# Triangular masks by position on GpSimd instead of multiplications on VectorE and ScalarE

## The chip, the cores and the metric

The kernel runs on one core of a Trainium2 chip. Time is device time in microseconds (us) from start to end of one execution. Engines are named as in the profile: PE (TensorE matmul), PEld (its weight load), DVE (VectorE), ACT (ScalarE), POOL (GpSimd), SP (SyncE, which issues most DMAs).

## The reference

The reference is a trunk of two layers over a sequence of 512 tokens with 1024 features, in float32. Layer 0 mixes tokens with an RWKV-7 recurrence, layer 1 with a gated block mixer; each is followed by a SwiGLU feed-forward net. The change touches the recurrence alone:

```python
def _rwkv7_scan(r, w, k, v, a, b):
    # S_t = S_{t-1} diag(w_t) + (S_{t-1} a_t) b_t^T + v_t k_t^T ;  y_t = S_t r_t
    def step(S, inp):
        r_t, w_t, k_t, v_t, a_t, b_t = inp
        sa = jnp.einsum('bhij,bhj->bhi', S, a_t)
        S = (S * w_t[:, :, None, :]
             + sa[..., None] * b_t[:, :, None, :]
             + v_t[..., None] * k_t[:, :, None, :])
        y = jnp.einsum('bhij,bhj->bhi', S, r_t)
        return S, y
...
x = x + _rmsnorm(h, norm_gains[i, 1])
```

There are 16 heads of 64 features. The kernel doesn't step through 512 tokens; it cuts them into 8 chunks of 64. Inside a chunk, what token s gives to token t is a product of two 64x64 tiles of which only the part with s before t counts (or s up to t, for the output). These products have to be masked to a triangle, and a unit triangular matrix has to be inverted.

## The kernel before, in words

The trunk runs recurrence, feed-forward, mixer, feed-forward in one program. The recurrence works on four blocks b of four heads. A list of stages at line 33, `PLAN`, sets in which order they are written: projections P, E (decay and scaled keys), then for each block F (front), B (back), S (scan of the state over the chunks) and N (norm, gate). The text order isn't the order of execution: the framework schedules all instructions with a model of their times, engine by engine, so a changed instruction can move others.

**front(b)** (line 677) handles four units, one per half of the chunks and pair of heads, and in each both heads. For a head it makes four products of 128x128 (L708, tile `lm`) into one PSUM bank; there are two such banks in turn, which `bkt` shares. `lm` holds for four chunks the two products, 64 by 2 by 64 values on 64 rows each for "other" (the rows of the other head) and "rows" (its own). From this bank four things are read: L711 multiplies the rows of the other head by the mask `mk2` (0 and 1; strict triangle for the first product, with the diagonal for the second) into the tile `MV` on DVE; L714 copies the upper part of the own rows' first product into `LA` on ACT in two copies of 32 rows, where the rest was zeroed ahead by POOL (L694); L715 copies the second product into `BX`. After both heads L716 multiplies that part of `BX` by the mask with the diagonal, on DVE. Then four transposes into `bkt` (L721) are copied to `BX` by ACT (L725, L726).

**back(b)** (line 729) transposes `LA` in blocks of 32 on DVE into `LX` (L734), and ACT scales a part of `LA` by a column of the mask, 0 or 1 per row (L739), beside POOL's zeroing of another part (L741). DVE then runs an elimination of 15 steps (L747, L749) on `LX` and `Dm` and transposes its result (L752, L753). From there small products on PE (`Qp` L769 first, which reads the changed `LA`, then `Np`, `Tp`, `Q2p`, `T2p`) put the inverse together, `mp` and `gh` apply it to `MV` and `BX` (L810, L817), and DVE adds the results into `MV` (L819, L820).

The mask is built at the start by one memset and four selects on POOL (L404 to L408). A select (`affine_select`) keeps an element where a linear function of its row and of its place in the row passes a comparison, and writes a constant elsewhere.

Of the kernel before, what the change touches and what calls it, by code (L numbers as in the profile page):

```python
# [7 lines left out]
F32 = mybir.dt.float32  # L8
F32R = mybir.dt.float32r
I32 = mybir.dt.int32  # L10
AF = mybir.ActivationFunctionType
ALU = mybir.AluOpType

P = 128
# [5 lines left out]
C = 64  # L20
# [62 lines left out]
class Trunk:  # L83
# [287 lines left out]
    def rwkv(self, x0, nxt):  # L371
        nc, i, tc = self.nc, self.i, self.tc
        v, a, g = nc.vector, nc.scalar, nc.gpsimd
        mm = nc.tensor.matmul
        with ExitStack() as ctx:
            ep = ctx.enter_context
            rp = ep(tc.tile_pool(name="rp", bufs=1))
# [12 lines left out]
            def e2(name, shape=(P, 2, T), dt=F32):  # L390
                return rp.tile(list(shape), dt, name=name, tag="e2", bufs=E2)

            def s4(name, shape, dt=F32):
                return self.slot(shape, dt, name)
# [5 lines left out]
                return self.gp.tile(shape, F32, name=name, tag="gain", bufs=2)  # L400


            mk2 = rp.tile([P, 2, C], F32, name="mk2")
            g.memset(mk2, 1.0)  # L404
            for r in (0, 64):
                for j, op in ((0, ALU.is_gt), (1, ALU.is_ge)):
                    g.affine_select(out=mk2[r:r + 64, j, :], in_=mk2[r:r + 64, j, :], compare_op=op,
                                    fill=0.0, base=0, pattern=[[1, C]], channel_multiplier=-1)  # L408
            rmask = rp.tile([P, NC, C], mybir.dt.bfloat16, name="rmask")
            g.memset(rmask, 1.0)  # L410
            g.memset(rmask[:, :, 0:1], 0.0)
# [85 lines left out]
            for t, m, w in ((w1m[0], omix, v), (w1m[1], self.vec["mix"], g)):  # L497
                mv = m[:, 3 * KT:5 * KT].rearrange("p (j k) -> p k j", j=2).unsqueeze(3)
# [109 lines left out]
            def early(b, k, r):  # L608
# [65 lines left out]
                        nc.sync.dma_start(out=sb[b][head[hd], :, :, n, :].rearrange("p q c t -> p (q c) t"), in_=sv(t)[head[hd]])  # L674
                return dict(pc=pc, BN=BN)

            def front(b, o):

                MV, ST, BX = {}, {}, {}
                for hh in range(2):  # L680
                    st = ST[hh] = e2("ST", (P, 2, 4, 2, C))
                    nc.sync.dma_start(out=st.rearrange("p q c n t -> p q (c n t)"),
                                      in_=sb[b][:, :, 4 * hh:4 * hh + 4].rearrange("p q c n t -> p q (c n t)"))
                    for q in q2:
                        mv = MV[hh, q] = s4("MV", [P, 2, 4, 2, C])
                        for hd in range(2):
                            g.memset(mv[head[1 - hd], :, :, hd], 0.0)
                            for n in range(2):
                                nc.sync.dma_start(out=mv[head[hd], n, :, hd],
                                                  in_=sa[b][n, head[hd], q, 4 * hh * C:4 * hh * C + 4 * C].rearrange("p (c t) -> p c t", t=C))  # L690
                LA = e2("LA", (P, 2, NC, C))
                Dm = self.f0p.tile([P, 2, 528], F32, name="Dm", tag="f0", bufs=2)
                for hd in range(2):
                    g.memset(LA[64 * hd + 32:64 * hd + 64, :, :, 0:32], 0.0)  # L694
                g.memset(full(Dm), 0.0)
                g.memset(Dm.rearrange("p b r -> p (b r)")[:, 0:1024:33], 1.0)
                for hh, q in units:
                    st, mv = ST[hh][:, q], MV[hh, q]

                    bx = BX[hh, q] = s4("BX", [P, 4, 4, C])  # L700
                    for hd in range(2):
                        nc.sync.dma_start(out=bx[head[hd], 2 + hd],
                                          in_=self.ident[head[hd], head[hd]].unsqueeze(1).broadcast_to([64, 4, C]))
                    for hd in range(2):
                        rows, other = head[hd], head[1 - hd]
                        lm = self.bank("pl", "lm")
                        for cc in range(4):
                            mm(lm[:, cc * P:(cc + 1) * P], st[:, cc].rearrange("p n t -> p (n t)"), mv[:, :, cc, hd, :], start=True, stop=True)  # L708
                        lv = lm.rearrange("p (c a t) -> p c a t", c=4, a=2)
                        la = LA[:, q, 4 * hh:4 * hh + 4]  # L710
                        v.tensor_tensor(mv[other, :, :, hd].rearrange("p a c t -> p c a t"), lv[other],  # L711
                                        mk2[other].unsqueeze(1).broadcast_to([64, 4, 2, C]), op=ALU.mult)
                        for z, x in ((64 * hd, 0), (64 * hd + 32, 32)):
                            a.copy(la[z:z + 32, :, x:C], lv[z:z + 32, :, 0, x:C])  # L714
                        a.copy(bx[rows, 1], lv[rows, :, 1, :])  # L715
                    v.tensor_tensor(bx[:, 1], bx[:, 1], mk2[:, 1:2, :].broadcast_to([P, 4, C]), op=ALU.mult)  # L716

                    sf = st.rearrange("p c n t -> p c (n t)")
                    pt = self.bank("pl", "bkt")
                    for cc in range(4):  # L720
                        nc.tensor.transpose(pt[:, cc * P:(cc + 1) * P], sf[:, cc], self.ident)  # L721
                    pv = pt.rearrange("p (c h f) -> p c h f", c=4, h=2)
                    for hd in range(2):
                        rows, other = head[hd], head[1 - hd]
                        a.copy(bx[rows, 0], pv[rows, :, hd])  # L725
                        a.copy(bx[other, 2 + hd], pv[other, :, hd])  # L726
                o.update(MV=MV, BX=BX, LA=LA, Dm=Dm)

            def back(b, o):

                MV, BX, LA, Dm = (o[n] for n in ("MV", "BX", "LA", "Dm"))
# [3 lines left out]
                LAu = LA.rearrange("p q c t -> p (q c) t")  # L735

                for r in (0, 64):
                    for z, x in ((r, 0), (r + 32, 32)):
                        a.activation(LAu[z:z + 32, :, x + 16:x + 32], LAu[z:z + 32, :, x + 16:x + 32], AF.Copy,  # L739
                                     scale=mk2[z:z + 32, 0, x + 16:x + 17])  # L740
                        g.memset(LAu[z:z + 32, :, x:x + 16], 0.0)  # L741
                LXd, Dmd = diag(LX), diag(Dm)
                for j in range(15):
                    n = 15 - j
# [53 lines left out]
                for u in range(16):  # L798
                    for hd in q2:
                        z = 64 * hd  # L800
                        mm(T2p[z:z + 32, u * 32:(u + 1) * 32], Q2[z + 32:z + 64, u, :], bdT[z + 32:z + 64, u, hd, 32:64],
                           start=True, stop=True)
                for hd, cp in ((0, a.copy), (1, v.tensor_copy)):
                    z = 64 * hd
                    cp(bdT[z:z + 32, :, hd, 32:64], T2p[z:z + 32, :].rearrange("p (u t) -> p u t", t=32))

                for hh, q in units:
                    mp, mt, mv, bx = self.bank("mp" if b else "pt", "mp"), MVt[hh, q], MV[hh, q], BX[hh, q]
# [4 lines left out]
                    for hd in range(2):  # L813
                        rows, other = head[hd], head[1 - hd]
# [132 lines left out]
            for n in PLAN:  # L947
                f, b = n[0], int(n[1])
                if f == "P":
                    if xr is None:  # L950
                        xr = mixed_split(0, "ssssssss")
                        xx.clear()
                    kr[b] = kr_proj(b)
                elif f == "E":
                    ops[b] = early(b, *kr[b])
                elif f == "X":
                    xs = mixed_split(2, XV)
                elif f == "V":
                    v_proj(xs, [b])
                elif f == "F":  # L960
                    front(b, ops[b])
                elif f == "B":
                    back(b, ops[b])
                elif f == "S":
                    if b == 3:
                        GW.append(gate_weights(b))
                        OB.extend(bonus(b, ops[b]))
                    Y[b] = scan(b, ops[b], (lambda y: finish_half(b, ops[b], y, (0, 1))) if b == 3 else None)
                elif b == 3:
                    finish_half(b, ops[b], Y[b], (2, 3))  # L970
                else:
                    finish(b, ops[b], Y[b])
# [166 lines left out]
```

## Time and profile before

| what | value |
|---|---|
| time, 3 runs | 1393.85 us (1392.23 to 1398.0) |
| the profiled execution: its time, its span | 1395.72 us, 1394.0 us |
| mean granted TensorE clock | 0.971 |
| PE, PEld, DVE, ACT, POOL busy | 1332.0, 1088.7, 783.9, 579.2, 152.6 us |
| first to last of the edited lines of the fronts and backs | some 187 to 352 us |

A row of a group reads: line, engine, operation, tile written <- tiles read, shapes, count | busy us in all, mean ns of one | idle time of the engine just before them and what ended it. In a timeline the first two numbers are start and length in us. A table by windows has for each stretch its length, then busy us and count for each engine asked for.

### The profile page before, as it was taken

Reading aid. Unit: us, or ns where it says so; the run is one execution under the profiler, and the core shown is the slowest. Engines: PE = TensorE matmul, PEld = TensorE weight load, DVE = VectorE, ACT = ScalarE, POOL = GpSimd, SP = SyncE. Lnnn points to the kernel's source line nnn. Section 1 sums busy time; section 2 is a strip of 40 time slices with the busy share of each in tenths; the row PEclk is TensorE's granted clock in tenths of the full one; section 3 lists DMA queues with packets and bytes.
Section 4 is the critical chain, followed back from the end, with each engine's and each line's share of the span. In section 5 each row is a group of like instructions: output and inputs, shape, how many; then the busy total and the mean of one; then the engine's idle time right before and its main releaser. Section 6 shows DMA issues by size and latency. Waiting matters only on the chain.

```text
span 1394.0 us, 21544 instructions
## 1 busy us (share of the span) xinstructions
PE 1332.0 (96%) x8512; PEld 1088.7 (78%) x8512; DVE 783.9 (56%) x1373; ACT 579.2 (42%) x1076; POOL 152.6 (11%) x190
## 2 busy tenths in 40 slices
PE   5999979989799899999999999999999999999998
PEld 3677768878687688888888887878888888888886
DVE  7975776579847565544553225575574554453223
ACT  5665765566543453222322224543463332232121
POOL 5000200111000021111110002010121111110000
PEclk8999979989799999999999999999999999999999
DMA  5145375432214233333322332342223333332231
GB/s 150 36 140 148 108 208 166 127 77 69 92 49 158 61 101 112 91 95 102 91 91 91 103 109 76 107 138 89 91 77 93 103 91 93 103 92 91 91 105 61
DMA packets 209956, 142.00 MB, mean 102 GB/s; under 512 B 59536, under 2 KB 185024, under 8 KB 209856
## 3 DMA queue, kind: packets, MB, share of 16 engines
q1 hardware_dynamic: 208560, 135.91, 33.0%
q0 software_dynamic: 1296, 4.72, 1.0%
q8 instruction: 67, 1.10, 0.3%
q14 instruction: 33, 0.27, 0.1%
HBM read 124.35 MB, written 14.16 MB: 99 GB/s over the span
## 4 chain that ended last, share of the span: by engine, by line
PE 62%; DVE 2%; ACT 0%; issue 0%; DVEq 0%
PE gu L157 12%; PE gu L158 12%; PE gu L156 11%; PE acc L157 8%; PE acc L158 8%; PE acc L156 8%; PE u L158 1%; PE u L157 1%; PE u L156 1%; DVE x L273 1%; PE s L1065 1%; PE ptr L218 0%; DVE hT L59 0%; DVE rt L208 0%; DVE ry L209 0%; DVE hn L270 0%
## 5 line engine op out<-in xcount | busy, mean ns | idle before, releaser
L131 ACT CAST whi<-wraw 128x1024 fp32r<-128x1024 f32 x177 | 185.7, 1049 | 481.3 <-PE gu L157 250.5
L132 DVE TENSOR_TENSOR wlo<-wraw,whi 128x1024 fp32r<-128x1024 f32 x177 | 263.1, 1487 | 206.3 <-ACT whi L131 202.3
L156 PE MATMUL gu<-hT,whi 128*128 128x512 f32 (+1 forms) x768 | 288.8, 378 | 1.8 <-ACT hT L57 1.7
L157 PE MATMUL gu<-hT,whi 128*128 128x512 f32 (+1 forms) x768 | 288.5, 377 | 1.1 <-DVE hT L59 1.1
L158 PE MATMUL gu<-hT,wlo 128*128 128x512 f32 (+1 forms) x768 | 289.5, 378 | 0.0
L156 PEld LDWEIGHTS gu<-hT,whi 128*128 128x128 f32 x768 | 145.0, 190 | 31.5 <-ACT hT L57 2.3
L157 PEld LDWEIGHTS gu<-hT,whi 128*128 128x128 f32 x768 | 144.9, 189 | 30.5 <-DVE hT L59 1.5
L158 PEld LDWEIGHTS gu<-hT,wlo 128*128 128x128 f32 x768 | 145.1, 189 | 28.5 <-issue 0.2
L157 PE MATMUL acc<-wlo,act 128*128 128x512 f32 x416 | 164.0, 394 | 0.0
L156 PE MATMUL acc<-whi,act 128*128 128x512 f32 x416 | 163.5, 394 | 0.0
L158 PE MATMUL acc<-whi,act 128*128 128x512 f32 x416 | 160.4, 394 | 0.0
L332 DVE TENSOR_TENSOR sg<-sg,gu 128x512 f32<-128x512 f32 x44 | 30.3, 688 | 142.2 <-PE gu L158 139.2
L333 POOL TENSOR_TENSOR sg<-sg,hn 128x512 f32<-128x512 f32 x44 | 57.0, 1295 | 417.3 <-DVE sg L332 417.3
L156 PEld LDWEIGHTS acc<-whi,act 128*128 128x128 f32 x416 | 78.2, 188 | 18.1
L158 PEld LDWEIGHTS acc<-whi,act 128*128 128x128 f32 x416 | 78.2, 188 | 18.0
L157 PEld LDWEIGHTS acc<-wlo,act 128*128 128x128 f32 x416 | 78.1, 188 | 18.0
L330 DVE TENSOR_TENSOR sg<-gu,hn 128x512 f32<-128x512 f32 x44 | 30.4, 691 | 66.5 <-PE gu L158 66.3
L131 ACT CAST act<-sg 128x512 fp32r<-128x512 f32 x52 | 32.3, 621 | 71.7 <-POOL sg L333 57.5
L156 PE MATMUL proj<-xsp,whi 128*128 128x512 f32 x128 | 51.6, 403 | 0.0
L158 PE MATMUL proj<-xsp,wlo 128*128 128x512 f32 x128 | 51.1, 401 | 0.0
L157 PE MATMUL proj<-xsp,whi 128*128 128x512 f32 x128 | 50.3, 396 | 0.2 <-DVE xsp L132 0.2
L708 PE MATMUL lm<-MV,ST 128*128 128x128 f32 x256 | 40.0, 309 | 7.0 <-ACT BX L726 3.0
(303 smaller groups left out, 2124.0 us busy)
## 6 DMA issues: line engine op xcount, KB each, us to landing
wraw<-in_ffn_w_gate_dram SPq DMA_DIRECT2D x44, 512.0 KB
wraw<-in_ffn_w_up_dram SPq DMA_DIRECT2D x44, 512.0 KB, 3.8
wraw<-in_ffn_w_down_dram SPq DMA_DIRECT2D x44, 512.0 KB, 3.7
wraw<-in_rwkv_w_rkv_dram SPq DMA_DIRECT2D x24, 512.0 KB, 3.7
wraw<-in_sgu_w_in_dram SPq DMA_DIRECT2D x16, 512.0 KB, 3.7
x<-in_x_dram SPq DMA_DIRECT2D x8, 512.0 KB, 3.2
MV<-sa SPq DMA_DIRECT2D x64, 64.0 KB, 2.5
ST<-sb SPq DMA_DIRECT2D x8, 512.0 KB
```

The source lines that it names most:

```text
L131: self.nc.scalar.copy(hi, src)
L132: self.nc.vector.tensor_tensor(lo, src, hi.bitcast(F32), op=ALU.subtract)
L156: mm(out, lhs[0], rhs[0], start=start, stop=False)
L157: mm(out, lhs[0], rhs[1], start=False, stop=False)
L158: mm(out, lhs[1], rhs[0], start=False, stop=stop)
L273: v.scalar_tensor_tensor(xts[tt][:, c], f, y[:, 0:1], xts[tt][:, c], op0=ALU.mult, op1=ALU.add)
L330: nc.vector.tensor_tensor(sg, pp[0], yb, op=ALU.mult)
L332: nc.vector.tensor_tensor(sg, sg, pp[1], op=ALU.mult)
L333: nc.gpsimd.tensor_tensor(sg, sg, yb, op=ALU.mult)
L708: mm(lm[:, cc * P:(cc + 1) * P], st[:, cc].rearrange("p n t -> p (n t)"), mv[:, :, cc, hd, :], start=True, stop=True)
L1065: mm(acc[:, tt * P:(tt + 1) * P], vt[tt][:, m * P:(m + 1) * P], wsT[:, m, :], start=True, stop=True)
```

## The change

The tile `mk2` and what built it are gone. A helper, `upper`, selects on POOL by position, in place in SBUF: of 64 rows with four groups of 64 elements it keeps the triangle and writes 0 elsewhere. ACT now copies all of the `lm` bank without mask, 64 rows each: the other head's rows into `MV` (128 values in four chunks), the own rows into `LA` and `BX`. POOL then selects in `MV` twice (each product), in `LA` and in `BX`, once for each head. In the back the scaling by a mask column on ACT is a select on POOL, of 32 rows by 256 elements.

```diff
@@ rwkv
-            mk2 = rp.tile([P, 2, C], F32, name="mk2")
-            g.memset(mk2, 1.0)
-            for r in (0, 64):
-                for j, op in ((0, ALU.is_gt), (1, ALU.is_ge)):
-                    g.affine_select(out=mk2[r:r + 64, j, :], in_=mk2[r:r + 64, j, :], compare_op=op,
-                                    fill=0.0, base=0, pattern=[[1, C]], channel_multiplier=-1)
...
+            def upper(t, base):
+
+                g.affine_select(out=t, in_=t, compare_op=ALU.is_ge, fill=0.0, base=base, pattern=[[0, 4], [1, C]],
+                                channel_multiplier=-1)
+
@@ front
-                for hd in range(2):
-                    g.memset(LA[64 * hd + 32:64 * hd + 64, :, :, 0:32], 0.0)
...
-                        v.tensor_tensor(mv[other, :, :, hd].rearrange("p a c t -> p c a t"), lv[other],
-                                        mk2[other].unsqueeze(1).broadcast_to([64, 4, 2, C]), op=ALU.mult)
-                        for z, x in ((64 * hd, 0), (64 * hd + 32, 32)):
-                            a.copy(la[z:z + 32, :, x:C], lv[z:z + 32, :, 0, x:C])
+                        a.copy(mv[other, :, :, hd].rearrange("p a c t -> p c a t"), lv[other])
+                        for n in range(2):
+                            upper(mv[other, n, :, hd], n - 1)
+                        a.copy(la[rows], lv[rows, :, 0, :])
+                        upper(la[rows], -1)
                         a.copy(bx[rows, 1], lv[rows, :, 1, :])
-                    v.tensor_tensor(bx[:, 1], bx[:, 1], mk2[:, 1:2, :].broadcast_to([P, 4, C]), op=ALU.mult)
+                        upper(bx[rows, 1], 0)
@@ back
-                        a.activation(LAu[z:z + 32, :, x + 16:x + 32], LAu[z:z + 32, :, x + 16:x + 32], AF.Copy,
-                                     scale=mk2[z:z + 32, 0, x + 16:x + 17])
+                        later = LAu[z:z + 32, :, x + 16:x + 32]
+                        g.affine_select(out=later, in_=later, compare_op=ALU.is_ge, fill=0.0, base=15,
+                                        pattern=[[0, 16], [0, 16]], channel_multiplier=-1)
                         g.memset(LAu[z:z + 32, :, x:x + 16], 0.0)
```

The line numbers of the changed kernel are lower by 2 to 6: the copies are L708 (MV), L711 (LA) and L713 (BX), the select is L673, LX is L732, the select of the back L738, the elimination L746 and L748.

The scheduler puts the instructions in another order. On ACT, in the first front, each read of a product waited for DVE before (number of the buffer behind each name; in brackets the semaphores waited for):

```order
L714 COPY LA_1510<-lm_1519 32x256 [waits DMAHW6_49,DVE_49]
L714 COPY LA_1510<-lm_1519 32x4x32
L715 COPY BX_1516<-lm_1519 64x256
L649 ACT_TABLE_LOAD
L649 ACTIVATE tw_1351<-tw_1351 128x1024 [waits Activation_49]
L725 COPY BX_1516<-bkt_1538 64x256 [waits PE_49]
L726 COPY BX_1516<-bkt_1538 64x256
L725 COPY BX_1516<-bkt_1538 64x256
L726 COPY BX_1516<-bkt_1538 64x256
L714 COPY LA_1510<-lm_1528 32x256 [waits DVE_49]
```

Now the first read of a bank waits for PE itself, and for POOL, which zeroed the tile MV:

```order
L708 COPY MV_1474<-lm_1511 64x4x2x64 [waits PE_49,Pool_49]
L711 COPY LA_1504<-lm_1511 64x256 [waits DMAHW6_49]
L713 COPY BX_1508<-lm_1511 64x256
L708 COPY MV_1474<-lm_1523 64x4x2x64 [waits PE_49,Pool_49]
L711 COPY LA_1504<-lm_1523 64x256
L713 COPY BX_1508<-lm_1523 64x256
```

Both heads' products of a unit are read on end, three copies for each; ACT waits for no engine but PE and POOL there.

On POOL the first front had nothing to do but zeroing; the last rows of it and the first of the back stood so:

```order
L694 MEMSET LA_1510 32x16x32 [waits DMAHW6_49,DVE_49,Pool_49]
L694 MEMSET LA_1510 32x16x32
L695 MEMSET Dm_1511 128x1024 [waits DMAHW0_49,DMAHW3_49,DVE_49,DMAHW5_49,Activation_49,Pool_49]
...
L741 MEMSET LA_1510 32x16x16 [waits DVE_49]
L741 MEMSET LA_1510 32x16x16 [waits Activation_49]
```

Now the end of that front and the start of the back read, in POOL's own order:

```order
L673 AFFINE_SELECT BX_1580<-BX_1580 64x256 [waits Activation_49]
L692 MEMSET Dm_2093 128x1024 [waits DVE_49,PE_49,Pool_49]
L693 MEMSET Dm_1505 128x32
L673 AFFINE_SELECT MV_1497<-MV_1497 64x4x64 [waits Activation_49,Pool_49]
L673 AFFINE_SELECT MV_1497<-MV_1497 64x4x64
L673 AFFINE_SELECT LA_1504<-LA_1504 64x256 [waits Activation_49]
L673 AFFINE_SELECT BX_1616<-BX_1616 64x256 [waits Activation_49]
...
L673 AFFINE_SELECT BX_1616<-BX_1616 64x256 [waits Activation_49]
L738 AFFINE_SELECT LA_1504<-LA_1504 32x16x16 [waits DVE_49]
L740 MEMSET LA_1504 32x16x16
```

A memset of the next block's Dm (Dm_2093) stands among the selects of the first block, and the selects of the last head lie ahead of the back's.

On DVE, around the LX of the last block, masks stood on both sides of it:

```order
L752 STREAM_TRANSPOSE hn<-Dm 128x32x32
L753 STREAM_TRANSPOSE Dt<-Dm 128x32x32
L716 TENSOR_TENSOR BX<-BX,mk_128 128x256
L711 TENSOR_TENSOR MV<-lm,mk_128 64x4x2x64
L848 TENSOR_TENSOR su<-us,pc 64x2x64
L132 TENSOR_TENSOR g2l<-g_4780,g2h 128x256
L711 TENSOR_TENSOR MV<-lm,mk_128 64x4x2x64
L772 TENSOR_TENSOR Qs<-Qp,id_147 128x512
L734 STREAM_TRANSPOSE LX<-LA 128x1024
L875 TENSOR_REDUCE mu<-Y 128x16
L716 TENSOR_TENSOR BX<-BX,mk_128 128x256
L132 TENSOR_TENSOR wlo<-wraw,whi 128x1024
```

Now the same place reads:

```order
L751 STREAM_TRANSPOSE hn<-Dm 128x32x32
L752 STREAM_TRANSPOSE Dt<-Dm 128x32x32
L847 TENSOR_TENSOR su<-us,pc 64x2x64 x3
L771 TENSOR_TENSOR Qs<-Qp,id_141 128x512
L132 TENSOR_TENSOR g2l<-g_4846,g2h 128x256
L847 TENSOR_TENSOR su<-us,pc 64x2x64
L732 STREAM_TRANSPOSE LX<-LA 128x1024
L746 TENSOR_TENSOR tm<-LX,Dm 128x2x15
L748 TENSOR_TENSOR Dm<-Dm,tm 128x2x15
L746 TENSOR_TENSOR tm<-LX,Dm 128x2x28
```

No mask is left, and the elimination starts directly behind LX.

## The prediction

> **What bounds the kernel now.** I read the page first, then the chain of waits, then a table by stretches of time.
>
> ```profile
> span 1394.0 us, 21544 instructions
> PE 1332.0 (96%) x8512; PEld 1088.7 (78%) x8512; DVE 783.9 (56%) x1373; ACT 579.2 (42%) x1076; POOL 152.6 (11%) x190
> PE 62%; DVE 2%; ACT 0%; issue 0%; DVEq 0%
> ```
>
> TensorE is busy for 96% of the span, and it alone makes up nearly all that the chain followed back from the end shows. So a mask that another engine does can only be worth the time in which TensorE stands still, or runs at a low granted clock, because of it. The table by stretches says where that is (columns: length, then busy time and instructions of PE, PEld, DVE, ACT and POOL, granted clock, DMA share, GB/s).
>
> ```profile
> 185.00:215.00 30.00, 22.46 (x152) 20.26 (x151) 23.20 (x30) 18.12 (x44) 3.28 (x7) 0.77 0.75 201
> 215.00:262.00 47.00, 43.86 (x744) 42.45 (x744) 25.51 (x55) 23.80 (x52) 2.32 (x6) 0.93 0.39 123
> 262.00:313.00 51.00, 45.28 (x793) 40.28 (x791) 36.86 (x82) 35.10 (x93) 10.02 (x22) 0.90 0.45 116
> 313.00:348.00 35.00, 33.39 (x425) 28.33 (x424) 31.63 (x90) 23.01 (x66) 4.75 (x12) 1.00 0.28 68
> 348.00:380.00 32.00, 24.09 (x412) 19.98 (x411) 28.60 (x67) 17.02 (x31) 1.22 (x4) 0.68 0.31 96
> 505.00:1394.00 889.00, 878.56 (x3978) 717.61 (x3978) 422.50 (x620) 291.08 (x462) 88.46 (x68) 1.00 0.31 95
> ```
>
> From 505 us on TensorE is busy for 878.6 of 889 us at a clock of 1.00, and no edited line runs there: nothing is to be had. The edited work lies in 185 to 380, the fronts and backs of the four blocks. Two places have slack on TensorE. In 185 to 215 (the first front) it is idle for 7.5 of 30 us, at a clock of 0.77. In 313 to 380 (the last front and back) DVE is the fullest engine, 60.2 of 67 us, and TensorE is idle for 1.6 us ahead of 348 and 7.9 us behind it. Between them, 215 to 313, TensorE is busy for 89.1 of 98 us and no other engine is near full.
>
> **The change part by part.** The groups of 185 to 380, by shape, carry the durations (count, then busy us, mean ns, idle before and what ended it):
>
> ```profile
> L711 DVE TENSOR_TENSOR MV<-lm,mk 64x512 f32<-64x512 f32 x32 | 22.0, 687 | 9.0 <-PE lm L708 8.4
> L716 DVE TENSOR_TENSOR BX<-BX,mk 128x256 f32<-128x256 f32 x16 | 6.7, 417 | 4.8 <-ACT BX L715 4.8
> L714 ACT COPY LA<-lm 32x256 f32<-32x256 f32 x32 | 11.6, 361 | 21.7 <-DVE MV L711 21.4
> L714 ACT COPY LA<-lm 32x128 f32<-32x128 f32 x32 | 8.2, 258 | 0.4
> L715 ACT COPY BX<-lm 64x256 f32<-64x256 f32 x32 | 11.8, 367 | 3.0 <-DVE MV L819 2.1 <-PE Yp L859 0.2 <-PE v L158 0.2
> L725 ACT COPY BX<-bkt 64x256 f32<-64x256 f32 x32 | 11.7, 365 | 5.4 <-PE bkt L721 5.4
> L763 ACT COPY MVt<-mvt 128x512 f32<-128x512 f32 x12 | 6.9, 584 | 2.7 <-PE mvt L760 1.6 <-PE gh L817 0.9
> L739 ACT ACTIVATE LA<-LA,mk 32x256 f32<-32x256 f32 x16 | 8.1, 505 | 2.9 <-DVE LX L734 2.7
> L741 POOL MEMSET LA<- 32x256 f32 x16 | 4.9, 305 | 37.7 <-DVE LX L734 37.1
> L687 POOL MEMSET MV<- 64x512 f32 x16 | 8.3, 521 | 44.7 <-DVE MV L819 34.9 <-PE Yp L859 9.2 <-PE v L158 0.2
> ```
>
> DVE loses both masks: 22.0 + 6.7 = 28.7 us. ACT loses L714 (11.6 + 8.2) and L739 (8.1), 27.9 us. It gains 32 copies of 64x256 into LA, at L715's 0.367 us 11.7 us, and 32 copies of 64x512 into MV, which L763's copy of the same length prices at 0.584: 18.7 us. ACT ends 2.5 us heavier, but no longer stands behind DVE's masks for 21.4 us (the L714 row).
>
> GpSimd gets 128 selects of 64x256 and 16 of 32x256, and loses small memsets. The only selects in this trace are at its start:
>
> ```profile
> L407 POOL TENSOR_SCALAR_AFFINE_SELECT mk<-mk 64x64 f32<-64x64 f32 x4 | 0.8, 235 | 0.0
> masks.py:199 POOL TENSOR_SCALAR_AFFINE_SELECT ident<-ident 128x128 f32<-128x128 f32 x1 | 0.3, 285 | 0.1
> L404 POOL MEMSET mk<- 128x128 f32 x1 | 0.2, 202 | 0.0
> ```
>
> From 64 to 128 elements a row a select grows by 50 ns, 0.78 ns an element, so one of 256 takes 285 + 128 x 0.78 = 385 ns; I take 0.39. The lower bound is that of the memset of 256, 0.305 (L741). The upper bound is that each of the four rows of 64 in the new pattern costs a select of its own, 4 x 0.235 = 0.94. 0.39 is what two rows of the same instruction give, so I stay with it: 144 x 0.39 = 56 us of GpSimd, in a stretch of 195 us in which it was busy for 3.28 + 2.32 + 10.02 + 4.75 + 1.22 = 21.6.
>
> **First front, 187.2 to 212.9.** The chain here runs lm product, mask on DVE, three copies on ACT, and back for the next of two banks:
>
> ```profile
> 186.26 1.95 PE L708 MATMUL lm<-MV,ST 128*128 128x128 f32 x16
> 192.91 3.75 PE L708 MATMUL lm<-MV,ST 128*128 128x128 f32 x16 [3.04 <-ACT BX L726]
> 187.19 1.06 ACT L648 ACTIVATE tw<-tw 128x1024 f32<-128x1024 f32 x1 [1.70 <-DVE tw L647]
> 189.18 1.28 ACT L649 ACT_TABLE_LOAD   x1
> 204.61 1.05 ACT L131 CAST whi<-wraw 128x1024 fp32r<-128x1024 f32 x1
> 212.87 2.05 DVE L734 STREAM_TRANSPOSE LX<-LA 128x1024 f32<-128x1024 f32 x1 [0.77 <-ACT LA L714]
> ```
>
> Now ACT alone sets the pace. Per product 0.584 + 0.367 + 0.367 = 1.32 us, eight of them 10.5; 16 copies of bkt at 0.366, 5.9; two activations of 1.06, one table load of 1.28 and two casts of 1.05, 5.5: 21.9 us. Behind the last copy GpSimd has two selects of MV, which run beside ACT's copy of LA, and one of LA: some 0.8 us. So LX starts 22.7 us behind 187.2 instead of 25.7: 3 us gained, within the 7.5 us in which TensorE is idle. The v products that filled the holes of this front come later now, under the elimination on DVE that follows; I count no gain and no loss for them.
>
> **Middle, 215 to 313.** The ACT waits vanish too, but no wait of TensorE hangs on them but once (3.04 us, above). I count nothing; the bound is the 8.9 us in which TensorE is idle.
>
> **Last front and back, 313 to 380.** Asked by line, the two masks are there with
>
> ```profile
> 313.00:380.00 67.00, 6.18 (x9) 0.85 0.29 81
> 313.00:380.00 67.00, 2.08 (x5) 0.85 0.29 81
> 314.57 1.95 DVE L734 STREAM_TRANSPOSE LX<-LA 128x1024 f32<-128x1024 f32 x1
> 348.47 1.96 DVE L734 STREAM_TRANSPOSE LX<-LA 128x1024 f32<-128x1024 f32 x1
> 374.42 2.08 DVE L752 STREAM_TRANSPOSE hn<-Dm 128x1024 f32<-128x1024 f32 x1
> ```
>
> so 8.3 us of the fullest engine go. All but 0.4 us of it lies ahead of the LX at 348.5, and there TensorE is idle for 1.6 us only: LX comes 1.6 us earlier, more only if products move behind it. Behind LX the elimination shares DVE with the norm of the earlier blocks, and some rows of block 2 that stood ahead of LX now follow it; neither shrinks. I take 2 us of the 8.3.
>
> **The rest.** After the LX transpose four selects and four memsets alternate on GpSimd, 4 x (0.39 + 0.305) = 2.8 us, where ACT's four activations took 4 x 0.505 = 2.0 us. The reader is the Qp product behind the elimination, some 30 us later (LX at 348.5, its transposes at 374.4): hidden; without that cover it would be 0.8 us a block. The five instructions that built the mask, 4 x 0.235 + 0.202 = 1.1 us, lie on GpSimd ahead of any product: nothing. What queues behind a waiting select on GpSimd is the next block's memsets of Dm and MV, and LX, the one tight reader, waits behind both.
>
> **Sum.** 3 + 0 + 2 = 5 us off the profiled execution's 1395.72 us (1.7 us of it outside the span of 1394.0). That execution is 1.9 us above the median, 1393.85, so the time is 1393.85 - 5 = **1389 us**.
>
> **Two engines at one memory.** This speaks against the change: other GpSimd instructions that read SBUF held DVE up, or were held up by it. Below them stand DVE's two lines of the elimination in 313 to 380 (L747, then L749).
>
> ```profile
> 525.26 1.92 DVE L132 TENSOR_TENSOR wlo<-wraw,whi 128x1024 fp32r<-128x1024 f32 x1 [0.54 <-ACT whi L131]
> 524.80 1.30 POOL L333 TENSOR_TENSOR sg<-sg,hn 128x512 f32<-128x512 f32 x1 [7.50 <-DVE sg L332]
> L132 DVE TENSOR_TENSOR wlo<-wraw,whi x177: 1201/1226/2377, 18.7 to 1366.1; 128x1024 fp32r<-128x1024 f32 x177
> L77 POOL TENSOR_SCALAR hn<-ident,y x12: 599/610/1540, 499.5 to 1029.8; 128x128 f32<-128x128 f32 x12
> 313.00:380.00 67.00, 7.42 (x30) 0.85 0.29 81
> 313.00:380.00 67.00, 7.48 (x30) 0.85 0.29 81
> ```
>
> The split that takes 1.226 us at the median took 1.92 beside a GpSimd product that ran from 524.80 to 526.10, and a one-input GpSimd instruction of 0.610 reached 1.540 us. No select ran beside DVE in this trace, so its case is unseen. Bounds for 313 to 380: 9 of the 32 masks of L711 stand there, so 9/32 x 128 = 36 selects, and 8 more of two backs, 44 x 0.39 = 17.2 us. At one end nobody waits; at the other DVE waits for all 17.2. About half of the work left to DVE there could be touched at all: the elimination's 14.9 us read two tiles of SBUF (LX or Dm with tm), while the six transposes, some 12 us, read one, and the products with mp, gh and us read a product of TensorE. Part of the waiting would fall on GpSimd instead, as in L77's row. So I take a fourth, 4 us, and it comes out of the 8.3 - 2 = 6.3 us of DVE's relief that I have not counted: it costs nothing. The Trainium skill, page "SBUF — State Buffer", section "Who interferes with whom", states that a DVE instruction with two SBUF inputs and a GpSimd instruction that reads SBUF shut each other out, one blocked until the other is done; the lengthened split agrees, and by that rule the elimination's 60 instructions would be the ones to lengthen.
>
> **The rivals.**
>
> *The full relief comes out.* DVE's 8.3 us all shorten 313 to 380, because products of TensorE move behind LX into the 7.9 us of idling there, and the clock of 0.68 rises with it. With 3 us of the front and a third of the middle's 8.9, 14 us: **1380**. For it: DVE is busy for 31.63 of 35 and 28.60 of 32 us, more than ACT by 8 and 11. Against it: TensorE's 33.39 of the same 35 us.
>
> *Selects hold DVE up.* In 313 to 380 its two-input instructions wait for them: 17.2 - 8.3 = 9 us more where DVE is fullest, and the first front's 3 us go the same way: **1403**. It decides from 8.3 / 0.39 = 21 of the 44 selects, if each holds DVE for its whole length. For it: the rows above. Against it: the half of DVE's work that reads one tile.
>
> *A select costs 0.94 us.* In the first front 32 of them take 30 us, where the front took 25.7: 4 us lost. Between the last two LX, 348.47 - 314.57 = 33.9 us, GpSimd would have 36 x 0.94 + 12 memsets (4 x 0.305 and 8 x 0.521, 5 in all) = 39 us: 5 more lost. With no relief left, 9: **1403**. It decides from (33.9 - 5) / 36 = 0.80 us a select. Against it: two rows with the same instruction.
>
> *Nothing moves.* The front's 3 us is work of TensorE that only shifts, so the total of its products sets the time: **1394**.
>
> **How the numbers follow.** A difference of 0.5%, 7 us, is about what a measurement of this kernel can tell from none: faster means below 1386.9, slower above 1400.8. Chances: forecast 0.37, full relief 0.34, selects that hold DVE up 0.15, costly selects 0.06, nothing moves 0.08. Of the forecast's share 0.05 falls below 1386.9. Faster: 0.34 + 0.05 = 0.39. Same: 0.32 + 0.08 = 0.40. Slower: 0.15 + 0.06 = 0.21. The range goes from 1377, 3 us below the full relief, to 1407, 4 above the two slower cases; I leave 0.1 out on each side, full relief with more of the idle time in it below, and the slower cases together above. The forecast's own range is 1385 to 1394.
>
> **What would show it.** Selects of 64x256 near 0.39 us. No ACT copy waiting for a DVE mask, against 21.4 us. The first block's LX some 23 us behind the activation of tw that stands at 187.19, against 25.7, and TensorE idle for less than 7.5 us in that front. The last block's LX 3 to 5 us earlier in all, and from it to the elimination's end as long as now. L747 and L749 at a mean of 0.25 us as now (7.42 / 30); at 0.35 or more the selects hold DVE up. If the stretch that is now 505 to the end is not 889 us long, something other than these steps is in it. The forecast is wrong if LX waits for GpSimd by more than 2 us in a block, or if the last Qp comes over 8 us earlier.

## The result, and the profile after

The changed kernel is slower: 1409.21 us median of five executions (1403.7 to 1412.82) against 1396.79 for the kernel before (1392.23 to 1398.0), a ratio of 1.0098 with a 95% interval of 1.008 to 1.0116, some 13 us. The profiled execution of it took 1403.7 us, the fastest of its five (granted clock 0.974, the others 0.968 to 0.971), so the traces show 8 us of the difference, not all of it.

First the page of the changed kernel, then its table by stretches (the columns are those of the table in the prediction).

```profile
span 1402.0 us, 21623 instructions
PE 1330.4 (95%) x8512; PEld 1087.2 (78%) x8512; DVE 766.0 (55%) x1325; ACT 579.2 (41%) x1060; POOL 215.5 (15%) x321
```

```profile
0.00:185.00 185.00, 165.19 (x787) 120.07 (x788) 139.39 (x215) 112.45 (x182) 27.51 (x53) 0.99 0.42 117
185.00:215.00 30.00, 21.79 (x158) 18.42 (x157) 16.05 (x17) 23.70 (x50) 22.02 (x36) 0.89 0.79 214
262.00:313.00 51.00, 42.30 (x712) 37.67 (x710) 32.29 (x76) 33.87 (x87) 26.96 (x64) 0.90 0.48 121
313.00:348.00 35.00, 34.21 (x442) 29.89 (x441) 23.52 (x60) 20.18 (x53) 17.39 (x45) 0.90 0.24 60
348.00:380.00 32.00, 23.98 (x453) 20.25 (x453) 24.57 (x63) 18.67 (x38) 8.11 (x19) 0.75 0.27 85
505.00:1402.00 897.00, 885.13 (x4041) 723.61 (x4039) 427.82 (x652) 299.66 (x493) 92.02 (x72) 1.00 0.31 95
```

The relief is there: DVE has 23.52 us of work from 313 to 348 where it had 31.63, and ACT stands behind no DVE mask. GpSimd now works for 22 of 30 us in the first front. But the first row is the one to look at. Ahead of 185 us no mask is applied in either kernel, and yet TensorE was busy there for 165.19 us with 787 products (clock 0.99), in the kernel before for 168.81 with 792 (clock 0.95):

```profile
0.00:185.00 185.00, 168.81 (x792) 123.43 (x793) 138.71 (x215) 114.46 (x184) 28.57 (x60) 0.95 0.44 123
```

When the same step starts in the two profiled executions, by their timelines (us):

| step | before | changed | later by |
|---|---|---|---|
| first v product (the projections are done) | 156.7 | 160.5 | 3.8 |
| first lm product | 186.3 | 188.0 | 1.7 |
| LX of the four blocks | 212.9, 269.8, 314.6, 348.5 | 213.8, 272.3, 316.3, 354.1 | 0.9, 2.5, 1.7, 5.6 |
| Qs of the last block | 393.7 | 397.5 | 3.8 |
| last gh product ends | 426.5 | 434.8 | 8.3 |
| first gu product (the feed-forward net) | 487.7 | 496.0 | 8.3 |

From there to the end of the last product both take the same time, 899.6 and 899.2 us. So the loss lies ahead of 435 us, in several pieces, and some of it where nothing was edited but the order.

The new instructions themselves, in groups and in the waits of 185 to 400:

```profile
L673 POOL TENSOR_SCALAR_AFFINE_SELECT MV<-MV 64x256 f32<-64x256 f32 x64 | 29.9, 489 | 73.4 <-ACT MV L708 73.1
L673 POOL TENSOR_SCALAR_AFFINE_SELECT LA<-LA 64x256 f32<-64x256 f32 x32 | 15.7, 492 | 2.0
L673 POOL TENSOR_SCALAR_AFFINE_SELECT BX<-BX 64x256 f32<-64x256 f32 x32 | 14.7, 459 | 21.2 <-ACT BX L713 20.9
L738 POOL TENSOR_SCALAR_AFFINE_SELECT LA<-LA 32x256 f32<-32x256 f32 x16 | 10.1, 632 | 4.4 <-DVE LX L732 3.5
```

```profile
DVE LX L732 <- POOL LA L673: 6.9, 3, 4.4
```

GpSimd waits for ACT most of the time (73.1 us ahead of the selects of MV). LX waits for a select for 6.9 us in all. That is a wait that was not there before, so selects and order are two suspects.

### The profile page after: what moved, and what is told of

Its sections match the earlier page's. It is cut to its first block, busy times and chain, and to the rows that moved or that the text cites. A ratio compares the mean times of both kernels' runs of the same rounds, so it can differ in the third digit from the quotient of the medians.

```text
span 1402.0 us, 21623 instructions
## 1 busy us (share of the span) xinstructions
PE 1330.4 (95%) x8512; PEld 1087.2 (78%) x8512; DVE 766.0 (55%) x1325; ACT 579.2 (41%) x1060; POOL 215.5 (15%) x321
## 4 chain that ended last, share of the span: by engine, by line
PE 80%; DVE 7%; DMA 5%; ACT 4%; issue 3%; SPq 1%; POOL 0%; DVEq 0%; ACTq 0%; POOLq 0%
PE gu L158 11%; PE gu L156 11%; PE gu L157 11%; PE acc L156 9%; PE acc L157 8%; PE acc L158 8%; PE gh L816 2%; PE proj L156 2%; PE proj L158 2%; PE proj L157 2%; PE mp L809 1%; PE lm L705 1%; PE u L158 1%; PE u L157 1%; PE u L156 1%
## 5 line engine op out<-in xcount | busy, mean ns | idle before, releaser
L156 PE MATMUL proj<-xsp,whi 128*128 128x512 f32 x128 | 52.2, 412 | 0.9 <-ACT r L522 0.9
L148 POOL TENSOR_TENSOR wlo<-wraw,whi 128x1024 fp32r<-128x1024 f32 x12 | 29.0, 2420 | 138.1 <-ACT whi L147 138.1
```

The source lines that it names most:

```text
L148: nc.gpsimd.tensor_tensor(lo, raw, hi.bitcast(F32), op=ALU.subtract)
L156: mm(out, lhs[0], rhs[0], start=start, stop=False)
```

## The experiments

Theory A: the loss comes from the order in which the scheduler put all engines' instructions once a few of them had changed. Theory B: it comes from the selects, by their time on GpSimd, by LX waiting for them, by DVE held up by them.

To tell them apart, an order has to be held while the work changes. A few lines do that: behind the building of the program, each instruction of an engine gets an edge to the one that is to stand ahead of it. The edge sets the order of issue and waits for nothing. The table holds the places of the wanted order. Each run below has a ratio to the kernel before, timed beside it on the same chip; its median moved between 1395.5 and 1397.8 us from chip to chip, so a difference in us between two runs on different chips is good to some 2 us at best.

```diff
+def _pin(nc, tc, table):
+    ...
+    dep = mybir.DependencyInfo(mybir.DependencyClass.NoSync, mybir.DependencyReason.DATA)
+    for engine, steps in order.items():
+        at, last = 0, None
+        for s in steps:
+            at += s
+            i = per[engine][at]
+            if last is not None:
+                tc.add_manual_dep(i, last.name, dep, reason="order")
+            last = i
...
     with tile.TileContext(nc, schedule_with_timeline_sim=True) as tc:
         build(tc, ins, outs[0])
+        _pin(nc, tc, _ORDER)
```

### The work of the one in the order of the other

The changed kernel in the old order (`_ORDER` from the kernel before, for PE, DVE, ACT and SP):

> The changed kernel's instructions, but every instruction that both kernels have is held on PE, DVE, ACT and SP in the order in which the kernel before has it (edges that set only the order of issue); on ACT the copies into MV and LA stand where the two old copies into LA stood; the selects on GpSimd are free. Theory A (the loss comes from the new order that the scheduler made of all engines): 1386 to 1397 us, as before or up to 10 below. Theory B (the loss comes from the selects themselves: their time on GpSimd, LX waiting for them, DVE held up by them): 1404 to 1412, as the changed kernel.

The kernel before in the new order (`_ORDER` from the changed kernel, the masks of DVE left to the scheduler):

> The kernel before with its masks on DVE and ACT, but PE, ACT, SP and all of DVE except the masks held in the order that the changed kernel has. Theory A (order): 1404 to 1414 us, as slow as the changed kernel. Theory B (the selects themselves): 1393 to 1399, as before.

The first took 1395.51 us against 1397.75 for the kernel before on the same chip, 0.9982 (0.9966 to 0.9997). The second took 1415.25, 1.013 (1.0107 to 1.0154). Theory A, on both sides: with the old order the new masks cost nothing and may gain 2 us; with the new order the old masks are as slow as the new ones or slower (the intervals just overlap). In the old order LX waits for GpSimd no less, 8.0 us in all against 6.9:

```profile
DVE LX L732 <- POOL LA L673: 8.0, 4, 5.1
```

so that wait by itself does not make the difference.

### The selects left out, and doubled, in both orders

```diff
             def upper(t, base):
-                g.affine_select(out=t, in_=t, compare_op=ALU.is_ge, fill=0.0, base=base, pattern=[[0, 4], [1, C]],
-                                channel_multiplier=-1)
+                pass
...
-                        g.affine_select(out=later, in_=later, compare_op=ALU.is_ge, fill=0.0, base=15,
-                                        pattern=[[0, 16], [0, 16]], channel_multiplier=-1)
```

> The changed kernel in its own order on PE, DVE, ACT and SP, with all 144 selects left out, so that the products stay unmasked. Theory A (order): 1404 to 1412 us, since the waits that cost time are not for GpSimd. Theory B (the selects): 1399 or less, the whole loss of 10 to 12 us gone.

The other edit puts `for _ in range(2):` ahead of both selects.

> The changed kernel in its own order, with each of the 144 selects done twice in a row (the second changes nothing): 144 more instructions of about 0.45 us on GpSimd, 65 us. Theory A (order): at most 5 us above the changed kernel. Theory B (the selects): as much again as the selects are said to cost, 10 us or more above it, so 1419 or more.

Without selects, 1401.73 us, 1.0045 (1.0022 to 1.0068): 7.5 us of the changed kernel's loss went, not all of it. With each done twice, 1434.51, 1.0268 (1.0246 to 1.029): 25 us more. Theory A as I had put it, that the selects hardly matter, falls here: in the new order some half of the loss or more needs them (7.5 of 12.4 us, good to 4 us by the two intervals). The same pair in the old order settles what this price belongs to:

> As the run with the new work in the old order (1395.5 us), with all 144 selects left out, so that the products stay unmasked. Theory S (the selects cost about 7.5 us wherever they are, as they did in the new order, where leaving them out gave 1401.7 against 1409.2): 1387 to 1389 us. Theory T (they cost time only where the order puts them on the path of the front): 1393 to 1396.

> As the run with the new work in the old order (1395.5 us), with each of the 144 selects done twice. In the new order this cost 25 us. Theory S (a price that goes with the selects): 1417 to 1423. Theory T (the old order leaves GpSimd room between the products): at most 12 more, 1396 to 1408.

| order | selects left out | once | twice |
|---|---|---|---|
| new | 1401.7 | 1409.2 | 1434.5 |
| old | 1394.4 | 1395.5 | 1423.0 |

In the old order one set of selects costs 1 us, which can't be told from nothing (0.9988, 0.9972 to 1.0003 without, 0.9982 with). Theory T holds for one set. For two it falls: 27 us more, where I had expected at most 12, so the room on GpSimd ends between one set of selects and two. With doubled selects LX stands behind GpSimd:

```profile
DVE LX L733 <- POOL LA L674: 32.8, 4, 15.5
```

The table also parts the loss. With no select at all the new order costs 7.3 us (1401.7 against 1394.4), the selects alone, in the old order, 1.1, and the rest, some 6 us, comes only where both meet.

The run without selects in the old order says one thing more: with no mask on any engine the kernel takes 1394.4 us, 2 us under the kernel before (4 at the edge of the interval). In that order the masks on DVE were worth no more than that.

### Why the order changed: the five instructions at the start

Two edits leave the masks as they are and touch only what GpSimd does in the first 7 us. In the kernel before, the mask is built some lines later:

```diff
-            mk2 = rp.tile([P, 2, C], F32, name="mk2")
-            g.memset(mk2, 1.0)
-            for r in (0, 64):
-                ...
             rmask = rp.tile([P, NC, C], mybir.dt.bfloat16, name="rmask")
...
             g.memset(bdT, 0.0)
+            mk2 = rp.tile([P, 2, C], F32, name="mk2")
+            g.memset(mk2, 1.0)
+            for r in (0, 64):
+                ...
```

> The kernel before, with the five set-up instructions that build the mask on GpSimd moved some lines down, behind the other set-up memsets, and the scheduler left free: the same work, but the scheduler then lines up all engines anew. Theory A (what the scheduler's order happens to be is worth several us here, whatever is changed): 4 us or more away from the kernel before, most likely slower, 1401 to 1412. Theory C (only the order that the new masks bring is bad, a mere reshuffle costs nothing): within 3 us of it.

In the changed kernel, the mask that nobody reads any more is built again at its old place:

> The changed kernel, scheduler free, with the old mask still built at the start (five instructions on GpSimd that nobody reads). With them the order of all engines up to the first front is that of the kernel before again. Theory A, first part: the first v product starts at some 156.7 us again instead of 160.5, and the time falls by about 4, to 1405. If the start's delay is taken up later, the time stays at 1407 to 1412.

The old masks, with five set-up instructions moved: 1409.82 us, 1.0096 (1.0079 to 1.0113). That is as much as the whole loss of the change, without the change. In the traces this kernel and the changed one have the same order up to the first front, over TensorE's first 830 products; behind it the scheduler made another order for each, so that the two times agree so closely is chance. The new masks, with the mask still built: 1397.55, 1.0011 (0.9996 to 1.0026). The loss is gone; I had expected 1405 at best.

How five small instructions get there: the copies of `id` on ACT wait for a memset of GpSimd that stands behind the mask. First the kernel before, then the one with the mask built later:

```profile
3.37 0.90 ACT L425 COPY id<-ident 32x32 f32<-32x32 f32 x4 [1.08 <-POOL id L423]
```

```profile
2.26 0.90 ACT L419 COPY id<-ident 32x32 f32<-32x32 f32 x4
```

ACT is done with them 1.1 us sooner, and the rows that follow, the small steps of the first norm, stand in another order on ACT, DVE and PE. On the chip nothing is won by it: the norm's first step on ACT waits for the DMA of x and starts at 4.26 us, before at 4.29. PE's first rows, in the kernel before and the one with the mask built later:

```profile
7.88 1.09 PE L218 MATMUL ptr<-ident,hn 128*128 128x128 f32 x4 [7.88 <-DVE hn L442]
```

```profile
7.32 1.94 PE L218 MATMUL ptr<-ident,hn 128*128 128x128 f32 x8 [7.32 <-DVE hn L442]
```

That the scheduler's model of the times saw the same 1.1 us and chose by it is my reading; its model is not on record. What this does to the projections, 45 to 100 us, in the kernel before, the changed one, the one with the old masks built later and the one with the new masks and the mask built (each row from its own kernel's table):

```profile
45.00:100.00 55.00, 54.83 (x250) 39.93 (x249) 48.80 (x66) 39.45 (x57) 0.13 (x1) 1.00 0.36 102
```

```profile
45.00:100.00 55.00, 51.10 (x222) 35.67 (x221) 49.20 (x66) 37.20 (x54) 0.13 (x1) 0.97 0.36 98
```

```profile
45.00:100.00 55.00, 51.05 (x222) 35.71 (x221) 49.26 (x66) 37.28 (x54) 0.13 (x1) 0.97 0.35 98
```

```profile
45.00:100.00 55.00, 54.30 (x247) 39.22 (x246) 48.78 (x66) 39.46 (x57) 0.13 (x1) 1.00 0.35 101
```

Two pairs, and they pair by the start, not by the masks. Where the mask is not built first, TensorE is idle for 3.9 us of these 55, and waits mostly for the splits of DVE (in the changed kernel):

```profile
PE proj L158 <- DVE wlo L132: 1.9, 1, 1.9
PE proj L157 <- DVE xsp L132: 1.0, 2, 0.6
PE proj L156 <- ACT r L522: 0.9, 1, 0.9
```

### What the start costs itself, and what the order behind it

The part ahead of the first front has the same instructions in both kernels, so its order can be put in alone. The first run has the changed kernel's order with the old start; the second the kernel before with the new start.

> The changed kernel held in its own order, but the part ahead of the first front (the first 734 products on PE, 217 instructions on DVE, 168 on ACT, 108 on SP, the same ones in both) stands in the order of the kernel before. Theory D (the new start costs its own 4 us, v starts at 160.5 instead of 156.7, and the other 8 to 10 us come from the order behind it): about 1405 us. Theory K (the start alone carries the loss, by what arrives late behind it): 1396 to 1400.

> The mirror image: the kernel before, its masks on DVE, held in its own order, but the same part ahead of the first front stands in the order of the changed kernel. Theory D: 4 us above the kernel before, 1399 to 1401. Theory K: 1406 to 1411.

1404.13 us, 1.0071 (1.004 to 1.0103), and 1401.42, 1.0036 (1.0021 to 1.0052). By the medians the start is worth 5 us in each kernel, theory D; the remaining 8 or so come from the order behind it. In the kernel before the 5 us are clear of the noise. In the changed kernel they are less sure, as the intervals with and without the mend overlap (1.004 to 1.0103, 1.008 to 1.0116); theory K's 1400 at most is out.

In the order behind the start two waits stand out in the trace of the changed kernel. In the tail of the last block, casts of the output projection's inputs, which wait for DMAs, stand on ACT ahead of the two copies into Dn that the next product needs:

```profile
404.60 1.14 ACT L131 CAST oT<-oraw 128x512 fp32r<-128x512 f32 x2 [3.00 <-DMA oraw<-od]
405.76 1.16 ACT L783 COPY Dn<-Np 32x512 f32<-32x512 f32 x2
```

The product Np was done at 402.4. In the kernel before the copies start with it:

```profile
398.45 1.16 ACT L784 COPY Dn<-Np 32x512 f32<-32x512 f32 x2 [4.98 <-PE Np L778]
```

The edit of the order moves them ahead, and one copy on DVE with them:

```diff
 ACT
+L783 COPY Dn<-Np x2
 L131 CAST g2h<-g
 L131 CAST oT<-oraw x2
-L783 COPY Dn<-Np x2
 DVE
+L785 COPY bdT<-Tp
 L132 g2l<-g,g2h
 L132 oT<-oraw,oT x2
-L785 COPY bdT<-Tp
```

> The changed kernel held in its own order, but on ACT the two copies into Dn of the last block stand ahead of the three casts that wait for DMAs (g2h, oT), and on DVE one copy into bdT ahead of the three subtractions that follow these casts. Theory A, last part (3 us of the loss are Dn waiting behind these casts): 3 us below the changed kernel, 1406, and T2p of the last block some 3 us sooner behind its Qs. If this wait lies beside another, 1408 to 1410.

1405.77 us, 1.0063 (1.0044 to 1.0083), 3.4 us under the changed kernel. The number is the expected one, the mechanism is not. The copies into Dn did come sooner, 5.0 us behind the start of Qs instead of 8.3, but T2p, which I expected some 3 us sooner behind it, comes 16.3 us behind it instead of 16.5. The start of Qs and of T2p, in the changed kernel and with the mend:

```profile
397.49 0.69 DVE L771 TENSOR_TENSOR Qs<-Qp,id 128x512 f32<-128x512 f32 x1 [0.75 <-PE Qp L768]
413.97 0.24 PE L800 MATMUL T2p<-bdT,Q 32*32 32x32 f32 x2
```

```profile
394.64 0.69 DVE L771 TENSOR_TENSOR Qs<-Qp,id 128x512 f32<-128x512 f32 x1 [0.75 <-PE Qp L768]
410.95 0.24 PE L800 MATMUL T2p<-bdT,Q 32*32 32x32 f32 x2
```

The wait lay beside another, then: ahead of its last products of Tp TensorE stands still for 2.33 us without the mend and for 2.49 with it. And the profiled execution is ahead by 2.9 us at Qs already, before anything that was mended. The kernel with the new masks and the mask built has these copies just as late, 8.3 us behind Qs, and no loss. So this wait isn't shown to be any part of it.

The second wait lies between the second and the third LX. A DVE step stands ahead of a copy while its DMA is still under way (issued by SP at 301.75, landed 4.30 us later), so the copy is late, ACT waits for that copy, and TensorE, it seems, for a bank that ACT has not read: the last row names no releaser, but it starts 0.09 us after ACT's last copy from that bank ends (310.98).

```profile
306.08 1.29 DVE L892 TENSOR_TENSOR hn<-hn,bn 128x512 f32<-128x512 f32 x2 [4.74 <-DMA hn<-Vd]
307.79 0.67 DVE L785 COPY bdT<-Tp 32x512 f32<-32x512 f32 x1
308.50 0.58 ACT L785 COPY bdT<-Tp 32x512 f32<-32x512 f32 x1 [8.68 <-DVE bdT L785]
311.07 2.04 PE L705 MATMUL lm<-MV,ST 128*128 128x128 f32 x8 [3.58 <-issue]
```

All three mends at once, the old start, the tail's copies, and the copy into bdT ahead of the two steps of hn:

> The changed kernel held in its own order with three mends, all 144 selects in place: the part ahead of the first front in the old order (5 us in the run before), the tail's Dn copies ahead of the casts that wait for DMAs (3.4 us in its own run), and on DVE one copy into bdT of the second block ahead of the two multiplications of hn that wait 4.74 us for a DMA (behind it ACT waits 8.68 us, and TensorE 3.58 us for its next lm). If these three waits are the loss, and add up: 1409 - 5 - 3.4 - 3.5 = 1397 us, level with the kernel before (1394 to 1400). If the selects hold a part of it, or the waits lie beside one another: 1402 to 1406.

1399.86 us, 1.0025 (1.0005 to 1.0046): with all selects in place, 9 of the 13 us are back by the medians. The ten executions run from 1393.72 to 1408.94, and the interval overlaps with that of the old start alone, so the 4.3 us between the two can't be divided between the other two mends. The profiled execution is the slowest of the ten. In it TensorE is idle for 8.4 us between the second and third LX, 8.7 in the changed kernel, though ACT waits for the mended copy for 2.15 us instead of 8.68: DVE and ACT wait elsewhere in that stretch instead. From the last LX to Qs it takes 52.2 us at a granted clock of 0.64, where the changed kernel takes 43.4 at 0.80, so it is no fair picture of the median. The start's share is the one piece of the order that a run sets apart; the rest I can't lay to single waits.

### Looking for something better than both

LX first among the readers:

```diff
-                        a.copy(mv[other, :, :, hd].rearrange("p a c t -> p c a t"), lv[other])
-                        for n in range(2):
-                            upper(mv[other, n, :, hd], n - 1)
                         a.copy(la[rows], lv[rows, :, 0, :])
                         upper(la[rows], -1)
+                        a.copy(mv[other, :, :, hd].rearrange("p a c t -> p c a t"), lv[other])
+                        for n in range(2):
+                            upper(mv[other, n, :, hd], n - 1)
```

> As the run with the new work in the old order (1395.5 us), but for each product the copy and the select of LA come ahead of those of MV. LX, the reader that GpSimd makes wait for 8.0 us in four blocks there, then has one select ahead of it instead of three. If LX is on the path that sets the end: 2 to 4 us less, 1391.5 to 1393.5, and LX waits for less than 4 us. If not: 1394 to 1397.

> The changed kernel, scheduler free, with the old mask still built at the start (read by nobody) and the copy and the select of LA ahead of those of MV. The start is that of the kernel before; behind it the scheduler makes an order of its own once more. If the start's order decides, 1394 to 1399 us like the run with the mask still built alone (1397.6). If the order behind it decides as much, anywhere between 1390 and 1410.

In the old order 1394.61 us, 0.9993 (0.9978 to 1.0008). LX waits for GpSimd for 5.0 us instead of 8.0, where I had named less than 4 for the case that LX is on the path, and the time does not change. But LX itself hardly came sooner (the first at 211.7 instead of 212.3, the last at 344.3 instead of 344.5), so what an earlier LX would be worth there isn't shown. With the scheduler free and the mask built, 1395.03, 0.9992 (0.9977 to 1.0007). As in the other kernels whose scheduler was free, the time goes with the start: three with the old one lie at 1395 to 1398, two with the new one at 1409 and 1410. Both beat the changed kernel by 14 us and neither beats the kernel before. The only one whose interval lies below 1 is the new work in the old order, by 0.2%.

## Why the prediction was wrong, point by point

I forecast 1389 us within 1377 to 1407 and gave slower 0.21. It was 1409.

**The step that failed** is a sentence of "The rest": the five instructions that built the mask "lie on GpSimd ahead of any product: nothing". As work they are nothing. As an input to the scheduler they are the loss: moving them in the kernel before, with no other edit, gave 1409.82, and putting them back into the changed kernel gave 1397.55. Every term of my sum took all other instructions to stay in their places. I looked at the order around the fronts and LX, where the masks are; the first rows that differ stand among PE's first ten. None of the rivals was a reordering.

A second gap is in the same paragraph: LX "waits behind both", memsets and selects, without a price. In the new order the selects are worth 7.5 us (1401.73 without them), in the old order 1.1. My sign of being wrong did come: LX waited for GpSimd by 4.4 us in one block, where I had named 2. But the old order has 5.1 us in one block and no loss, so this sign doesn't point at the cause.

**505 to the end** was expected to be as long as before, and is: 899.6 and 899.2 us from the first gu product to the end of the last product.

**The price of a select** was nearly right: I took 0.39, and the median is 0.413. The 32-row ones of the back have a median of 0.502, not 0.39. With waiting, the means are 459 to 632 ns, 72 us in all instead of 56. Their minimum, median and longest in the changed kernel:

```profile
L673 POOL TENSOR_SCALAR_AFFINE_SELECT MV<-MV x64: 406/413/1391, 189.9 to 353.2; 64x256 f32<-64x256 f32 x64
L738 POOL TENSOR_SCALAR_AFFINE_SELECT LA<-LA x16: 494/502/1462, 216.0 to 360.1; 32x256 f32<-32x256 f32 x16
```

**Selects hold DVE up** was a rival at 1403, near the number and mostly the wrong reason. The mechanism is real: the elimination's steps beside a select reach twice their length. Their rows in the kernel before, then in the changed one:

```profile
L747 DVE TENSOR_TENSOR tm<-LX,Dm x60: 172/258/294, 215.2 to 372.9; 128x30 f32<-128x30 f32 x8, 128x56 f32<-128x56 f32 x8, 128x78 f32<-128x78 f32 x8, 128x96 f32<-128x96 f32 x8
```

```profile
L746 DVE TENSOR_TENSOR tm<-LX,Dm x60: 190/274/502, 216.9 to 377.5; 128x30 f32<-128x30 f32 x8, 128x56 f32<-128x56 f32 x8, 128x78 f32<-128x78 f32 x8, 128x96 f32<-128x96 f32 x8
```

Over the 87 DVE instructions that a select overlaps this adds 6.3 us to their undisturbed lengths (I had taken 4, for the last front and back alone); GpSimd loses 11 (72 less 128 x 0.413 and 16 x 0.502). This agrees with the exclusion that the Trainium skill states in "SBUF — State Buffer", section "Who interferes with whom". Where a long DVE step is under way it is the select that waits. But the same lengthening of DVE, some 6.5 us, is in the run with the old order, which is no slower than the kernel before. There it costs nothing.

**First front, 3 us gained.** From the first lm to LX it took 25.8 us, before 26.6; the forecast made that 23.6. Without selects it took 21.5. ACT's pace was counted about rightly; what I left out is that in the new order GpSimd, with 22.0 us of work in 30, is nearly as full as ACT and sets LX's start. In the old order it took 29.1 us, and 29.0 without selects.

**Last front and back, 2 us gained.** DVE's relief came, an earlier LX did not (354.1 instead of 348.5): TensorE was busy for 34.21 of 35 us ahead of it. That was the reason I gave against the full relief. The run with no mask at all puts the most that could come out of both places at 2 us in the old order, not 5.

## What to carry to other kernels

Where a scheduler orders a program, an edit's price has two parts, its work and the order that it sets off, and the second can be the far larger one: here the work cost 1 us in the old order and nothing that can be told from noise, the order 7 without any select and 14 with them, against the same kernel in the old one. Hold the order while the work is changed, or undo the edit's harmless part alone, before a cause is looked for in the work; compare the orders from their first row that differs, however far it lies from the edit. A forecast for such a kernel needs a rival for a reshuffle, with a price; here one was worth 13 of 1400 us. How often a reshuffle costs that much isn't known from this case.

## What the runs showed of the hardware that I had not expected

A select of 256 elements a row took 0.413 us at the median as four rows of 64 on 64 partitions, and 0.502 as sixteen rows of 16 on 32. If the rows of the pattern make the difference, they cost some 7 ns each (an estimate: 89 ns over twelve rows); no run here varied them alone. Beside DVE instructions of 1.3 us a select of 0.413 us grew to 1.39.
